# A two-layer encoder trunk on one core: an early gate row, deferred scans, gates split one block ahead, and other buffers for the last adaLN blocks

## The chip, the cores and the metric

The kernel runs on one core of a Trainium2 chip. The metric is the time of one execution in device microseconds (us), the median of several runs. The core has five engines with a queue each: TensorE (PE in the profile; PEld is its weight load), VectorE (DVE), ScalarE (ACT), GpSimd (POOL) and SyncE (SP), which issues most of the loads. An engine takes its queue in order. On-chip memory comes in tiles from pools with a fixed number of buffers. A compile-time scheduler orders the instructions of each engine, by their place in the program and by when it believes that their inputs and buffers are ready. Where the kernel sets an order by hand, the scheduler keeps it.

## The reference

512 tokens of width 1024 go through two layers. Each layer has a token mixer and a SwiGLU FFN of width 2816. Layer 0 mixes by stick-breaking attention with 16 heads, layer 1 by a gMLP with chunked position mixing. Every sub-layer is wrapped in RMSNorms and in adaLN, a shift, scale and gate computed from a condition vector c:

```
m = silu(c) @ w + b;  shift, scale, gate = split(m, 3)
h = rms_norm(x, pre_g) * (1 + scale) + shift
y = mixer(h)            # or swiglu(h)
x = x + gate * rms_norm(y, post_g)
```

In the attention, with z the scores of one head, a weight is beta of its own key times the product of (1 - beta) over the later keys; the kernel gets it as differences of a running product, which one scan along the row gives.

## The kernel before, in words

All matmuls are done in split fp32: an operand x becomes a high part (ACT, "split", L130) and a low part x - high (DVE), and three matmuls replace one (`mm3`, L122). So each weight block of 128x1024 costs one load, one ACT and one DVE instruction of about a microsecond each, and PE has three passes to cover them.

**Weights** come as one stream in the order of use (`stream`, L356 to L391). `wload` (L147) loads the next block into one of two raw buffers, `wemit` (L157) splits it into one of five, later six, buffers, and `wget` (L343) hands a block to the consumer and makes sure that some blocks ahead are emitted ("look", 3 unless told otherwise). The blocks of the FFN that are made of sums (`blocks`, L258) have a second raw block, `rawy`, in a pool of two buffers (tag `raw2`).

**General slots.** The pool `s4` (L45, `slot`, L58) has 28 buffers of 4 KB a partition for everything of middling life: activations, transposed inputs, FFN gates, gate sums, x tiles.

**adaLN in the background.** Three vectors (A scale, B shift, G gate) for each sub-layer are matrix-vector products of c with 1024x1024 blocks. The class `Bg` (L443) does them as a generator, a step at a time between other work: it loads eight blocks (`rawada`), adds each into an accumulator on DVE (`ada_stt`, L436), and at the end, in two halves of 512 columns, splits the accumulator (tiles `acch`, `accl`), sums over the partitions with a matmul against ones, and multiplies with the row of `pre_g` or `post_g` (tile `g`, loaded at that time to all partitions). `bg0` (L708) does G0, `bg` A0 and B0, and `bg2` (L1694) A2 and B2, the last ones. With `slots=0` the blocks go into the two `raw2` buffers, otherwise into general slots.

**Attention.** Heads are done in pairs, i = 0 to 7 (loop L1129 to L1167). In that stage PE and DVE are chained: each engine's instructions keep the program's order (`pe["chain"]`, `dve.chain`). `scores` (L1001) makes scores z, a sigmoid (ACT, tile `ga`) and the scan (DVE, tile `left`) for a group of key blocks: B31 (blocks 3 and 1), B2 and B0. `flip` (L1039) transposes scan blocks on PE (tile `tw`), takes them out on ACT and makes the low part on DVE (tiles `ar`). `values` (L1057) multiplies with the value differences U (tile `av`), `gather` (L1072) adds the two heads' halves (tile `of`), and `part` (L1082) splits the result (tile `o`). Pair i's iteration makes, in between, the scores of pair i+1; the scan of B0 is the last of them, just ahead of the last `values` and `gather`. LATE blocks need the scans of B31 and B2 only; EARLY ones need B0. Between the steps `fill` puts matmuls of the next q and k projections (`pqk`), or for the last pairs of the output projection (`y`). The sigmoid needs another ACT table than the square root of the norms; `sqrt_table` (L703) queues the reload behind `last_act`, the last instruction that needs the old table.

**Output projection and boundary.** `out_proj` (L618) is used after each sub-layer. It runs over the contraction blocks k; after the first FFN (`steps` = 2) the gate product of block k is split first (`act_split`, L1177, tile `as`), background steps are taken after each k, and token tile 0's sum is taken out halfway into `yp` and added at the end. The last four blocks are done token tile by token tile, followed by `boundary` (L539): norm, gate, residual, next norm, transposes on PE (tile `tp`), split (tiles `hTh`, `hTl`). At the end of tiles 2 and 3 the first products of the next sub-layer are put in (`nxt`): after the first FFN these are the v products of the gMLP (`v_first`, L1530), whose weights are `win_v` blocks. Inside tile 3's boundary (`mid`, L681) the flag `edge` orders the splits of `wgu` blocks behind that tile's square (ACT, `feature[1]`) and behind its normed x (DVE, `feature[0]`, tile `t`).

Of the kernel before, what the change touches and what calls it, by code (L numbers as in the profile page):

```python
# [35 lines left out]
def trunk(ctx: ExitStack, tc: tile.TileContext, A: dict, out: bass.AP):  # L36
# [120 lines left out]
    def wemit():  # L157
        n = len(got)
        src, a, b, key = stream[n]
        if len(raws) == n:  # L160
            wload()
        if key[0] == "vblocks":
            got.append(vblocks(raws[n]))
            return
        if src is None:
            if key[1][0] != "u" and (not first_blocks or n > first_blocks[-1] + KF):
                first_blocks.append(n)
            for _ in blocks(*next_raws(n)):
                pass
            return  # L170
        raw = raws[n]
        if key[0] == "wdn" and key[2] in SEVEN[key[1]]:
            got.append(down_blocks(raw))
            return
        h, l = wtile(a, b, SHORT if key[0] in ("wgu", "win_u") else 16)
        if key[0] == "wqk" and key[1]:

            act.activation(h[:], raw[:], AF.Copy)
            nc.vector.tensor_tensor(l[:], raw[:], h[:].bitcast(F32), ALU.subtract)
            if len(raws) == n + 1 and stream[n + 1][3][0] == "wqk":  # L180
                wload()
        else:
            high = act.activation(h[:], raw[:], AF.Copy)
            last_low[0] = nc.vector.tensor_tensor(l[:], raw[:], h[:].bitcast(F32), ALU.subtract)  # L184
# [258 lines left out]
    class Bg:  # L443
# [5 lines left out]
        def __init__(self, *parts, slots=0, lag=None, gap=2, flat=False):  # L449
            self.slots = slots  # L450
# [5 lines left out]
            self.parts = [  # L456
                (n, int(s), int(s) + (n != "G"), {"G": 2, "A": 1, "B": 0}[n]) for n, s in parts
            ]
            self.gen = self.run()

        def run(self):
            groups = [self.parts] if self.flat else [[p] for p in self.parts]
            for group in groups:
                raws = []
                n = KD * len(group)
                for j in range(n + self.lag):
                    if j < n:
# [16 lines left out]
            for name, at, s, part in self.parts:  # L484
                acc = ada[name, at]
                if part:
                    row = A["pre_g"] if part == 1 else A["post_g"]
                    g = slot(F32, "g", 1, D)[:, 0, :]
                    load(g, row[s : s + 1, :].to_broadcast([P, D]))
                for b in range(2):  # L490
                    c = slice(b * 512, (b + 1) * 512)
                    h = adas.tile([P, 512], F32R, tag="acch", name=nm("acch"))
                    l = adas.tile([P, 512], F32R, tag="accl", name=nm("accl"))
                    split(h[:], l[:], acc[:, c])
# [3 lines left out]
                    mm(ps[:], ones_r, h[:], True, False, last_tp[0])  # L498
                    mm(ps[:], ones_r, l[:], False, True)
# [39 lines left out]
    def boundary(s, tt, y, xin, hT, S, tag, mid=None):  # L539
# [4 lines left out]
        for hf, c in enumerate(halves):  # L544
            act.activation(junk[:, c], y[hf][:], AF.Square, accum_out=sq[hf][:])
            if hf == 1:
                sd, r2 = rms(sq[1][:], sq[0][:])
            dve.tensor_tensor(t[:, c], y[hf][:], ada["G", s][:, c], ALU.mult)
# [69 lines left out]
    def out_proj(s, nk, get_act, wkey, J, bg, hT, nxt=(), pre=None, S=None, steps=0, bg2=None):  # L618
# [23 lines left out]
        if pre is not None:  # L642
            npre = len(pre["w"])
            for tt in pre["y"]:
                y[tt] = pre["y"][tt]
        for k in range(nk - J):
            a = get_act(k)
# [14 lines left out]
            (k, get_act(k), wget(wkey(k), J + 1 if k == nk - J else 0))  # L662
# [5 lines left out]
        for tt in range(NT):  # L668
# [11 lines left out]
        for n, tt in enumerate((2, 3)):  # L680
# [5 lines left out]
            if nxt and tt == 2:  # L686
                evacs.append(nxt[0]())
            late.append(
# [19 lines left out]
    bg0, bg = Bg("G0", slots=3, gap=1), Bg("A0", "B0", lag=1, gap=1)  # L708
# [194 lines left out]
    with tc.tile_pool(name="att", bufs=1) as att, tc.tile_pool(name="att2", bufs=2) as att2:  # L903
# [80 lines left out]

        def attend(i):
# [15 lines left out]
            def scores(js):  # L1001
# [24 lines left out]
                if tri is None:  # L1026
                    tri = gaps[B0][0][:, : T - P * js[0]]
                    parts = [slice(o, o + T - P * js[0]) for o in at.values()]
                else:
                    parts = [slice(0, M)]  # L1030
                for c in parts:
                    dve.tensor_tensor_scan(r[:, c], g[:, c], tri, 1.0, ALU.mult, ALU.max)
                for h in range(2):
                    for j in js:
                        weights[h, j] = r, at[h, j]

            turned = {}

            def flip(blocks, h):  # L1039
# [10 lines left out]
                act.activation(ar[:, 0, :n], ps[:, :n], AF.Identity, bias=minus)  # L1050
# [78 lines left out]
        for i in range(NPAIR):  # L1129
# [4 lines left out]
            flip(LATE, 1)  # L1134
            if i:
# [24 lines left out]
            fill(next(F))  # L1160
            if more:
                cur[0](B0)
# [531 lines left out]
    bg2 = Bg("A2", "B2", lag=1, gap=3)  # L1694
# [110 lines left out]
```

## Time and profile before

| | us |
|---|---|
| median of 3 runs | 1102.92 (1102.55 to 1105.05) |
| profiled execution, its own time | 1103.49 |
| its span, first to last instruction | 1101.7 |
| PE busy in the span | 1082.1 |
| DVE busy | 972.8 |
| ACT busy | 610.1 |

The granted TensorE clock was 0.998 on the mean. Timeline rows give start, duration, engine, line, operation, tiles (out<-in), shape and count; in brackets stands the idle time before the row and what ended it. Rows that merge several instructions give the time from the first start to the last end. Since most operations go through helpers, rows are told apart by tiles, not by lines. A row of busy time by stretch gives, after the length, the busy time of PE, PEld, DVE, ACT and POOL with the number of instructions, then the granted clock, the busy share of the DMA engines and the GB/s that they moved. In the list of waits the numbers are the total, how often, and the longest.

### The profile page before, as it was taken

How to read it: one execution, taken by the hardware profiler on the slowest of the kernel's cores; microseconds unless marked ns; L12 is line 12 of the kernel's file. 1: busy time of each engine (PE TensorE's matmuls, PEld its weight loads, DVE VectorE, ACT ScalarE, POOL GpSimd, SP SyncE). 2: the span in 40 equal slices, each digit the busy share in tenths (PEclk: the TensorE clock that was granted, in tenths of full speed). 3: DMA queues.
4: the chain of work that ended last, by engine and by line, in shares of the span. 5: the costliest groups of instructions: out<-in, count | busy, mean ns of one | idle time of the engine just before them, and what ended most of it. 6: DMA issues, size and time to landing. Idle time of an engine off the chain costs nothing.

```text
span 1101.7 us, 18701 instructions
## 1 busy us (share of the span) xinstructions
PE 1082.1 (98%) x7452; PEld 978.7 (89%) x7452; DVE 972.8 (88%) x1293; ACT 610.1 (55%) x1016; POOL 29.5 (3%) x53
## 2 busy tenths in 40 slices
PE   7999999999999999999999999999999999999997
PEld 4787788788999999998888899988999999999996
DVE  4988999866989999989978999868979999899996
ACT  6554665665655555554252767526545555565662
POOL 0020100000000000001000000001000000000000
PEclk9999999999999999999999999999999999999999
DMA  8976434304433434359878324524334342332252
GB/s 317 357 226 218 138 121 131 122 17 153 153 111 124 163 124 153 134 187 347 294 246 322 143 87 137 177 95 163 122 113 153 136 159 100 107 113 96 77 190 78
DMA packets 51355, 176.38 MB, mean 160 GB/s; under 512 B 6074, under 2 KB 9146, under 8 KB 51268
## 3 DMA queue, kind: packets, MB, share of 16 engines
q1 hardware_dynamic: 48708, 166.81, 43.8%
q0 software_dynamic: 2560, 8.39, 2.1%
q8 instruction: 58, 0.95, 0.3%
q14 instruction: 29, 0.24, 0.1%
HBM read 164.69 MB, written 8.39 MB: 157 GB/s over the span
## 4 chain that ended last, share of the span: by engine, by line
PE 85%; DVE 7%; DMA 4%; issue 2%; ACT 2%; SPq 0%; DVEq 0%; ACTq 0%
PE r L111 35%; PE y L111 16%; PE pqk L111 7%; PE X L111 4%; PE gu L111 4%; PE Y L111 3%; PE v L111 3%; PE u L111 2%; PE av L111 2%; PE z L111 2%; PE tw L119 1%; PE Z L111 1%; PE W L111 1%; PE tp L119 1%; DVE wl L184 1%
## 5 line engine op out<-in xcount | busy, mean ns | idle before, releaser
L111 PE MATMUL r<-Sh,wh 128*128 128x256 f32 x640 | 177.3, 277 | 0.6 <-ACT e L89 0.6
L111 PE MATMUL r<-Sl,wh 128*128 128x256 f32 x640 | 177.0, 277 | 0.0
L111 PE MATMUL r<-Sh,wl 128*128 128x256 f32 x640 | 176.9, 277 | 0.0
L89 ACT ACTIVATE wh<-raw 128x1024 fp32r<-128x1024 f32 (+1 forms) x105 | 108.3, 1036 | 101.7 <-DMA raw<-in_wdown 36.1
L111 PE MATMUL y<-wh,as 128*128 128x512 f32 x480 | 150.5, 391 | 0.3 <-DVE svt L73 0.3
L111 PEld LDWEIGHTS r<-Sh,wh 128*128 128x128 f32 x640 | 120.2, 188 | 1.2 <-ACT e L89 1.0
L111 PEld LDWEIGHTS r<-Sl,wh 128*128 128x128 f32 x640 | 120.2, 188 | 0.1
L111 PEld LDWEIGHTS r<-Sh,wl 128*128 128x128 f32 x640 | 120.1, 188 | 0.0
L184 DVE TENSOR_TENSOR wl<-raw,wh 128x1024 fp32r<-128x1024 f32 x79 | 95.9, 1220 | 25.9 <-ACT wh L89 25.7
L73 DVE TENSOR_TENSOR wl<-f,wh 128x1024 fp32r<-128x1024 f32 x95 | 112.9, 1219 | 1.1 <-ACT wh L89 1.1
L89 ACT ACTIVATE wh<-f 128x1024 fp32r<-128x1024 f32 x95 | 100.2, 1055 | 17.3 <-DVE f L73 12.5
L111 PEld LDWEIGHTS y<-wh,as 128*128 128x128 f32 x480 | 90.0, 188 | 19.3 <-issue 0.6
L89 ACT ACTIVATE e<-r 128x256 f32<-128x256 f32 x120 | 45.9, 384 | 102.3 <-PE r L111 100.2
L111 PE MATMUL y<-wl,as 128*128 128x512 f32 x240 | 93.7, 391 | 0.0
L111 PE MATMUL r<-hTh,wh 128*128 128x256 f32 x320 | 88.8, 278 | 0.2 <-DVE gu L73 0.2
L111 PE MATMUL r<-hTh,wl 128*128 128x256 f32 x320 | 88.5, 277 | 0.0
L111 PE MATMUL r<-hTl,wh 128*128 128x256 f32 x320 | 88.5, 277 | 0.0
L111 PEld LDWEIGHTS r<-hTh,wh 128*128 128x128 f32 x320 | 60.1, 188 | 1.1 <-DVE gu L73 0.9
L111 PE MATMUL r<-hTh,b 128*128 128x256 f32 x320 | 60.9, 277 | 0.0
L111 PEld LDWEIGHTS r<-hTl,wh 128*128 128x128 f32 x320 | 60.1, 188 | 0.0
L111 PEld LDWEIGHTS r<-hTh,wl 128*128 128x128 f32 x320 | 60.1, 188 | 0.0
L89 ACT ACTIVATE wh<-rawx 128x1024 fp32r<-128x1024 f32 x40 | 42.5, 1062 | 29.7 <-PE r L111 28.9
(288 smaller groups left out, 2924.3 us busy)
## 6 DMA issues: line engine op xcount, KB each, us to landing
rawada<-in_ada SPq DMA_DIRECT2D x80, 512.0 KB, 6.3
rawy<-in_wy SPq DMA_DIRECT2D x38, 512.0 KB, 4.2
rawx<-in_wx SPq DMA_DIRECT2D x38, 512.0 KB, 3.4
raw<-in_wdown SPq DMA_DIRECT2D x22, 512.0 KB, 5.3
raw<-in_wdn SPq DMA_DIRECT2D x22, 512.0 KB, 3.4
raw<-in_wqk SPq DMA_DIRECT2D x16, 512.0 KB, 4.0
ada<-in_ada0p SPq DMA_DIRECT2D x12, 512.0 KB, 7.6
raw<-in_wgu SPq DMA_DIRECT2D x12, 512.0 KB, 3.5
```

The lines of the kernel that those rows point to most:

```text
L73: b = getattr(nc.vector, op)(*args, **kw)
L89: b = nc.scalar.activation(*args, **kw)
L111: b = nc.tensor.matmul(o, l, r, start=start, stop=stop, skip_group_check=True)
L119: last_tp[0] = nc.tensor.transpose(o, i, ident)
L184: last_low[0] = nc.vector.tensor_tensor(l[:], raw[:], h[:].bitcast(F32), ALU.subtract)
```

## The change

Six things are changed.

- **G0's row and halves** (`soon=True` for `bg0`). The row g is loaded right behind the eighth block instead of at the end. The two halves of the accumulator are split at once, the second into a general slot of its own.
- **Scans deferred.** For pairs 6 and 7 (made in iterations 5 and 6) the scan of B0 is left out of `scores` and done in the next iteration, behind both LATE flips and ahead of `last_part`.
- **Table reload later.** In the last iteration `last_act` is set to the last `ar` of the LATE flips, so the square-root table is loaded behind it.
- **Gates one block ahead.** In `out_proj` with `steps`, the gates of block k+1 are split before the weights of block k are asked for.
- **Last adaLN blocks in general slots.** `bg2` (`own=0`) takes general slots for its blocks.
- **Edges after the first FFN.** The two halves of `yp` are added inside the boundary as they are asked for, each with an order: the first behind the last weight's low part, the second behind DVE's instruction before it. `win_v` splits are ordered behind the boundary's square and normed x as `wgu` ones are, and the flag is also set for the products put in at tile 2.

```diff
-            if edge[0] and key[0] == "wgu":
+            if edge[0] and key[0] in ("wgu", "win_v"):
...
+        def row(self, name, s, part):
+
+            if part and name not in self.rows:
+                g = slot(F32, "g", 1, D)[:, 0, :]
+                row = A["pre_g"] if part == 1 else A["post_g"]
+                load(g, row[s : s + 1, :].to_broadcast([P, D]))
+                self.rows[name] = g
+            return self.rows.get(name)
...
-                        if self.slots:
+                        if self.slots or len(self.raws) >= self.own:
                             raw = slot(F32, "rawada", 1, D)[:, 0, :]
...
+                        self.raws.append(raw)
+                        if self.soon and j % KD == KD - 1:
+                            self.row(name, s, part)
...
+                g = self.row(name, s, part)
+                halves = []
                 for b in range(2):
                     c = slice(b * 512, (b + 1) * 512)
...
+                    if not (self.soon and b):
+                        h = adas.tile([P, 512], F32R, tag="acch", name=nm("acch"))[:]
+                        l = adas.tile([P, 512], F32R, tag="accl", name=nm("accl"))[:]
+                        split(h, l, acc[:, c])
+                        halves.append((h, l))
+                    if self.soon and not b:
+                        s = slot(F32R, "acc")
+                        split(s[:, 0, :], s[:, 1, :], acc[:, 512:])
+                        halves.append((s[:, 0, :], s[:, 1, :]))
+                    h, l = halves[b]
...
         for k in range(nk - J):
-            a = get_act(k)
+            a = act_at(k)
+            if steps:
+                act_at(k + 1)
             w = pre["w"][k] if k < npre else wget(wkey(k))
...
-                for hf in range(2):
-                    dve.tensor_tensor(yp[:, hf, :], y[tt][hf][:], yp[:, hf, :], ALU.add)
-                y[tt] = [yp[:, hf, :] for hf in range(2)]
+                ends = y[tt]
+
+                def added(hf):
+                    before = dve.prev if hf else last_low[0]
+                    b = dve.tensor_tensor(yp[:, hf, :], ends[hf][:], yp[:, hf, :], ALU.add)
+                    order(b, before)
+                    return yp[:, hf, :]
+
+                y[tt] = added
...
             if nxt and tt == 2:
+                edge[0] = steps > 0
                 evacs.append(nxt[0]())
+                edge[0] = False
...
-    bg0, bg = Bg("G0", slots=3, gap=1), Bg("A0", "B0", lag=1, gap=1)
+    bg0, bg = Bg("G0", slots=3, gap=1, soon=True), Bg("A0", "B0", lag=1, gap=1)
...
-            def scores(js):
+            def scores(js, later=False):
...
+                if not later:
+                    scan()
+                return scan
...
             flip(LATE, 0)
             flip(LATE, 1)
+            if scan is not None:
+                scan()
+            if not more:
+                last_act[0] = last_ar[0]
             if i:
                 last_part()
...
+            scan = None
             if more:
-                cur[0](B0)
+                scan = cur[0](B0, i > 4)
+                if i < 5:
+                    scan = None
...
-    bg2 = Bg("A2", "B2", lag=1, gap=3)
+    bg2 = Bg("A2", "B2", lag=1, gap=3, own=0)
```

`act_at(k)` is `get_act(k)` kept in a table, so that each block is split once; `scan()` holds the scan instructions that stood in `scores`.

More of the change, by code (lines that the diff above doesn't have):

```diff
@@ L983, in trunk @@
                 False: [att.tile([P, 544], F32, name=nm("left"))]}
+        last_ar, scan = [None], None
         def attend(i):
@@ L1035, in scores, with scan @@
                         weights[h, j] = r, at[h, j]
+                def scan():
+                    if tri is None:
+                        ones = gaps[B0][0][:, : T - P * js[0]]
+                        parts = [slice(o, o + T - P * js[0]) for o in at.values()]
+                    else:
+                        ones, parts = tri, [slice(0, M)]
+                    for c in parts:
+                        dve.tensor_tensor_scan(r[:, c], g[:, c], ones, 1.0, ALU.mult, ALU.max)
+                if not later:
+                    scan()
+                return scan
             turned = {}
```

37 lines of the change are left out of this document (15 added, 22 removed).

## The prediction

> **What bounds the kernel now.** I read the page's busy times, then busy time by stretch, then the list of what TensorE (PE) waited for, then the timelines around those waits.
>
> ```profile
> PE 1082.1 (98%) x7452; PEld 978.7 (89%) x7452; DVE 972.8 (88%) x1293; ACT 610.1 (55%) x1016; POOL 29.5 (3%) x53
> ```
> ```profile
> 0.00:25.00 25.00, 16.95 (x77) 9.59 (x77) 10.03 (x27) 16.39 (x32) 1.19 (x6) 1.00 0.82 318
> ...
> 1075.00:1100.00 25.00, 19.63 (x101) 16.48 (x99) 18.08 (x32) 5.61 (x16) 0.00 (x0) 0.93 0.24 81
> ```
> PE is idle for 1101.7 - 1082.1 = 19.6 us. The first 25 us hold 25 - 16.95 = 8.05 of it, the last stretch 5.37, the 1.7 us behind it all of theirs. Only 4.5 us of idle lie in the 1050 us between. No edit touches the two ends, so whatever the change gives comes out of these 4.5 us.
>
> ```profile
> PE av L111 <- DVE accl L73: 1.1, 1, 1.1
> PE av L111 <- DVE ar L73: 0.8, 1, 0.8
> PE r L111 <- ACT e L89: 0.6, 1, 0.6
> PE av L111 <- ACT ar L89: 0.4, 1, 0.4
> ...
> PE tp L119 <- DVE t L73: 0.3, 1, 0.3
> PE y L111 <- DVE svt L73: 0.3, 1, 0.3
> ```
> The list of waits names them (total, times, longest). Four lie where the diff works: accl (the background sum of gate G0), both ar waits (the last pairs of heads) and t (the boundary after the first FFN): 1.1 + 0.8 + 0.4 + 0.3 = 2.6 us. Idle time understates a stall, because a matmul's modelled end overlaps the next start; distances between starts show it whole:
>
> ```profile
> 93.59 0.40 PE L111 MATMUL pqk<-hTh,wl 128*128 128x512 f32 x1
> 93.82 0.39 PE L111 MATMUL av<-acch,ones 128*128 128x512 f32 x1
> 95.31 0.50 PE L111 MATMUL av<-accl,ones 128*128 128x512 f32 x1 [1.10 <-DVE accl L73]
> ```
> Neighbours start 0.23 apart, these two 1.49: the stall is 1.26 us, not 1.10.
>
> **The change, part by part.**
>
> *G0's row and halves.* On DVE:
>
> ```profile
> 87.78 0.69 DVE L73 TENSOR_TENSOR accl<-G,acch 128x512 fp32r<-128x512 f32 x1
> ...
> 93.97 0.69 DVE L73 TENSOR_TENSOR G<-av,g 128x512 f32<-128x512 f32 x1 [0.82 <-DMA g<-in_post_g]
> 94.58 0.68 DVE L73 TENSOR_TENSOR accl<-G,acch 128x512 fp32r<-128x512 f32 x1
> ```
> The second half's accl stands behind the product with g in DVE's written order, and that product waits for g's load. After, both halves are split together: the second accl comes 0.7 us behind the first, near 88.5, five us before PE asks. The 1.26 us go, even if g should come late. No instruction is added; the second pair of halves takes one general slot.
>
> The load of g (512 KB) moves up SP's queue, from 85.93 to behind the eighth block of G0:
>
> ```profile
> 42.88 4.25 SPq L128 DMA_DIRECT2D rawada<-in_ada  x5
> 55.62 2.70 SPq L128 DMA_DIRECT2D ones<-in_consts  x6
> ```
> ```profile
> 45.00:50.00 5.00, 4.77 (x21) 3.62 (x20) 4.86 (x9) 1.68 (x3) 0.00 (x0) 1.00 1.03 416
> ...
> 55.00:60.00 5.00, 5.00 (x23) 4.13 (x22) 4.96 (x5) 1.98 (x4) 3.05 (x8) 1.00 0.39 98
> ```
> SP issues nothing from 47.1 to 55.6, so no queue slot is taken from anyone. The DMA engines are full (share 1.03) until 50; at 416 GB/s the row takes 0.524 MB / 416 = 1.26 us. I cost it at nothing: the blocks ahead of it are only for G0's sum, which is done long before its accl at 87.78, and from 55 the share is 0.39. Without that cover it would be 1.26 us, once. [...] From 47 on g holds a general slot that A's blocks or the q and k tiles may want; PE waits for none of these before 93.
>
> Does PE's lead of 1.26 us survive? DVE is its partner through the eight pairs of heads, and it is nearly full. The tightest place, and the next one at which DVE waits:
>
> ```profile
> 125.13 1.02 DVE L73 SCALAR_TENSOR_TENSOR ar<-tw,ar 128x384 fp32r<-128x384 f32 x2
> ...
> 145.38 2.30 DVE L73 TENSOR_TENSOR_SCAN left<-ga,ones 128x1027 f32<-128x1027 f32 x1 [1.07 <-ACT ga L89]
> ```
> ```profile
> 126.99 1.08 PE L111 MATMUL av<-ar,U 128*128 128x128 f32 x8
> ```
> DVE's first ar ends near 125.65 and PE reads it at 127.1; the second ends at 126.15 and is read near 127.6. Slack 1.4 against 1.26: it holds, by a little. At 145 DVE waits 1.07 us for ACT's sigmoid of PE's scores, which would come earlier; DVE follows PE again from there. I carry the lead at its full 1.26.
>
> *Scan of pair 6 deferred.* Before:
>
> ```profile
> 216.39 2.28 DVE L73 TENSOR_TENSOR_SCAN left<-ga,ones 128x1025 f32<-128x1025 f32 x1
> ...
> 220.00 1.02 DVE L73 SCALAR_TENSOR_TENSOR ar<-tw,ar 128x384 fp32r<-128x384 f32 x2
> ...
> 224.56 1.02 DVE L73 SCALAR_TENSOR_TENSOR ar<-tw,ar 128x384 fp32r<-128x384 f32 x2
> ```
> ```profile
> 217.34 1.05 ACT L89 ACTIVATE ar<-tw,oneb 128x384 fp32r<-128x384 f32 x2
> ```
> ```profile
> 219.61 0.22 PE L111 MATMUL av<-ar,U 128*128 128x128 f32 x1
> 220.62 1.08 PE L111 MATMUL av<-ar,U 128*128 128x128 f32 x7 [0.79 <-DVE ar L73]
> ...
> 225.97 1.08 PE L111 MATMUL av<-ar,U 128*128 128x128 f32 x8
> ```
> The eight av matmuls start 0.11 apart; the second comes 1.01 late to the first: a stall of 0.90. With the 2.28 us scan behind it, DVE's ar follows ACT's at 218.4 and is done by 219.4, before PE's 219.7: the 0.90 go. But the scan is not gone. The timeline shows no pause of DVE between this scan and the next ar's end at 225.58, and the new order adds one, from the old start of the scan until ACT has delivered. PE, now 0.90 earlier, asks for that next ar near 225.1 instead of 225.97. So part is given back there: between nothing and all 0.90. I take the middle, a net 0.45.
>
> *Scan of pair 7 deferred, square-root table later.*
>
> ```profile
> 230.66 1.28 ACT L705 ACT_TABLE_LOAD   x1
> ...
> 233.19 1.05 ACT L89 ACTIVATE ar<-tw,oneb 128x384 fp32r<-128x384 f32 x2
> ```
> ```profile
> 233.00 0.40 PE L111 MATMUL y<-wh,o 128*128 128x512 f32 x1
> 233.83 0.33 PE L111 MATMUL av<-ar,U 128*128 128x128 f32 x1 [0.42 <-ACT ar L89]
> ```
> The table load sits ahead of the ar for which PE waits; the stall is 0.83 - 0.23 = 0.60. After, the load follows that ar, which comes 1.28 us sooner, and DVE's half no longer stands behind a scan. All 0.60 go. Next on ACT is the split of o, now 1.28 us behind the load; the output projection wants it only after the remaining fills. No further pair follows, so DVE owes nothing here.
>
> *Boundary after the first FFN.*
>
> ```profile
> 598.11 1.28 DVE L73 SCALAR_TENSOR_TENSOR B<-rawada,sc,B 128x1024 f32<-128x1024 f32 x1 [1.95 <-DMA rawada<-in_ada]
> ```
> ```profile
> 605.32 0.64 ACT L89 ACTIVATE b<-rawy 128x512 fp32r<-128x512 f32 x1 [1.45 <-DMA rawy<-in_wuy]
> ```
> The last blocks of A2 and B2 go through two buffers that the rawy loads share; DVE waits for them up to the edge, and a late rawy puts ACT's b in front of the square of x on which tile 0 hangs. In general slots both come sooner, and PE's wait for t goes: 0.26 (0.3 in the list). Adding the two halves of yp in turn keeps the order that DVE had anyway. Splitting the gates one block ahead: PE has no wait on them in this stage, nothing to win; two halves each on ACT and DVE (0.69 on DVE for this shape, as accl's row) move up one block, and one slot more is held. PE's block of 24 x 0.23 = 5.5 us hides them; without it, 1.4 us would show once, at the stage's start.
>
> *win_v's weights behind the boundary.* The block that tile 2's edge orders is no later than before. The last one is ordered by tile 3's:
>
> ```profile
> 625.17 1.21 DVE L184 TENSOR_TENSOR wl<-raw,wh 128x1024 fp32r<-128x1024 f32 x1
> ...
> 631.34 1.28 DVE L73 SCALAR_TENSOR_TENSOR t<-t,r,B 128x1024 f32<-128x1024 f32 x1
> ```
> ```profile
> 629.88 0.39 PE L111 MATMUL v<-wl,hTh 128*128 128x512 f32 x1
> ```
> PE reads this wl at 629.88. Behind t it ends at 632.62 + 1.21 = 633.83 if nothing else moves: 3.95 late. With the wl away, t itself comes about 1.2 sooner, so 2.75. Against that, this stretch of PE is not ordered by hand: v of token tile 2 (24 matmuls, 5.4 us) and u are ready work. Bounds 0 and 3.95; I take 0, the value of the nearest row: this read had no wait. Queued behind the waiting split are, on ACT, win_u's split and, on DVE, the sums of tiles 2 and 3; the raw buffer comes free later by as much, so SP's load of wvs behind it starts later too. PE needs none of these before it has used the last win_v block. The rest of the bound is a rival.
>
> **Sum.** 1.26 + 0.45 + 0.60 + 0.26 = 2.57 us. Against the profiled execution's own time, 1103.49 (its span of 1101.7 and 1.79 around it), that is 1100.9. That execution lies 0.57 above the median of the runs, 1102.92; from the median, 1100.4. With the give-back at its ends, 1099.9 to 1100.8; with some scatter of the schedule 1099.8 to 1101.2.
>
> **Rivals.** About 0.2% (2.2 us, a time under 1100.7) can be told from no change.
> 1. *win_v stalls PE.* For: the rows above. Against: ready work. If half covered, 1 to 2 us: 1101.4 to 1102.4. If PE's order was fixed without that cover, 4 to 5 us with the transposes of tile 3, which are ordered behind these matmuls: 1104.4 to 1105.4, slower than before. It decides above 2.6 us of stall.
> 2. *DVE eats the lead.* For: its slack is 1.4 us against 1.26, and it is full from 214. Then pair 6's 0.45 and pair 7's 0.60 are left of the first three terms, with the boundary 1.31: 1101.6.
> 3. *General slots run out.* SP stands in order behind a load without a buffer:
>
> ```profile
> 536.72 10.17 SPq L128 DMA_DIRECT2D rawada<-in_ada  x4
> ```
> ```profile
> raw<-in_wdown SPq DMA_DIRECT2D x22, 512.0 KB, 5.3
> ```
> SP stood 10.17 us over four such loads. A wdown load lands 5.3 us after its issue, and its two splits take about 1.2 each (wl above). Weights run three blocks ahead, 3 x 24 matmuls x 0.23 = 16.5 us, so 8.8 are spare. A slot of the gates comes free every two blocks, 11 us: a PE stall of about 2.2 us a time. Three of them take 6.6, and 1100.4 becomes 1107; it decides at two. Against: blocks of FFN gates come free all the while. [...]
> 4. *Neighbouring waits go too*, r's 0.6 and y's 0.3, as work shifts: 1099.5.
>
> **How the numbers follow.** Forecast 0.54 (two thirds of it below 1100.7); rival 1 covered by half 0.14, in full 0.06; rival 2 0.09; rival 3 0.06; rival 4 0.11. Faster: 0.37 + 0.11 = 0.48. Slower: half of the full rival 1, and rival 3: 0.09. Same: 0.43. The range runs from rival 4 with no give-back, 1099.0, to the upper half-covered rival 1 with the scatter of the runs, 1103.0.
>
> **What would show it.** Right: no PE wait on accl near 94; g issued near 47; the av wait of pair 6 gone and a small one near 225; the table load behind ar; tile 0's transposes without a wait. Wrong: a PE gap at v before 633, SP standing over 9 us in front of a wdown load, new ar waits between 100 and 215.

## The result, and the profile after

The kernel after takes 1110.36 us, the median of 6 executions (1108.83 to 1110.89), against 1103.91 (1102.15 to 1105.11) for the kernel before beside it: 1.0057 times as long, interval 1.0044 to 1.0070. The forecast was 1100.4, and a range of 1099.0 to 1103.0. The profiled execution took 1108.83, its span 1107.1.

The page's first line, then the list of what PE waited for (total, times, longest):

```profile
PE 1083.8 (98%) x7452; PEld 979.1 (88%) x7452; DVE 972.4 (88%) x1293; ACT 610.7 (55%) x1016; POOL 29.5 (3%) x53
```
```profile
PE v L111 <- ACT wh L89: 3.3, 1, 3.3
PE z L111 <- ACT ga L89: 1.5, 1, 1.5
PE tp L119 <- DVE t L73: 0.5, 1, 0.5
...
PE av L111 <- DVE ar L73: 0.2, 1, 0.2
```

PE's idle time is 1107.1 - 1083.8 = 23.3 us, 3.7 more than before. Of the four waits that were to go, accl's and ACT's ar are gone, DVE's ar is down to 0.2, t has grown. The two new ones together, 4.8, are larger than all that went, 2.1. Where the time went shows best when the same matmul is looked up in both traces (starts in us):

| matmul | before | after | difference |
|---|---|---|---|
| first score, z | 72.56 | 73.09 | +0.53 |
| 31st q and k fill | 95.65 | 94.82 | -0.82 |
| first transpose of pair 0's scans, tw | 102.45 | 101.66 | -0.79 |
| first av of the LATE blocks of pair 6 | 219.61 | 218.82 | -0.79 |
| first FFN product, gu | 277.47 | 277.50 | +0.02 |
| first y of the FFN | 493.85 | 492.70 | -1.15 |
| first v of the gMLP | 620.59 | 619.84 | -0.76 |
| last v | 646.88 | 652.59 | +5.71 |
| last of all | 1094.24 | 1099.57 | +5.34 |

The second last step holds the result: 6.47 us between the first and the last v. The timeline there (PE, ACT, DVE):

```profile
628.76 0.40 PE L111 MATMUL v<-wh,hTl 128*128 128x512 f32 x1
...
630.35 1.06 ACT L89 ACTIVATE junk<-x 128x1024 bf16<-128x1024 f32 x1 [1.95 <-DVE x L73]
...
631.40 1.04 ACT L89 ACTIVATE wh<-raw 128x1024 fp32r<-128x1024 f32 x1
...
632.50 1.22 PE L111 MATMUL v<-wh,hTh 128*128 128x512 f32 x2 [3.34 <-ACT wh L89]
```

PE has no v without win_v's last block; the high part, wh, stands behind the square of tile 3's x (junk), as the change orders it. Starts that would be 0.23 apart are 3.74 apart: 3.51 us. Busy time by stretch shows what follows; the number behind the five engines is the granted clock:

```profile
628.00:630.00 2.00, 1.16 (x5) 0.58 (x4) 2.00 (x4) 0.40 (x1) 0.00 (x0) 1.00 0.00 0
630.00:632.00 2.00, 0.00 (x0) 0.00 (x0) 2.00 (x4) 1.65 (x3) 0.53 (x1) 0.87 0.11 43
632.00:634.00 2.00, 1.50 (x3) 0.87 (x4) 1.95 (x4) 1.98 (x4) 0.00 (x0) 0.50 0.53 219
...
636.00:638.00 2.00, 2.00 (x6) 1.58 (x5) 0.42 (x1) 0.00 (x0) 0.00 (x0) 0.50 0.78 244
638.00:640.00 2.00, 2.00 (x9) 1.57 (x8) 0.00 (x0) 0.48 (x1) 0.00 (x0) 0.93 0.82 264
```

After the idle stretch the clock is 0.50 until 638, and v matmuls start 0.43 apart in place of 0.23: the starts between 632.50 and 638.4 hold 2.96 us more than at full clock. 3.51 + 2.96 = 6.47.

The other new wait is at the deferred scan of pair 6:

```profile
218.32 2.28 DVE L73 TENSOR_TENSOR_SCAN left<-ga,ones 128x1025 f32<-128x1025 f32 x1
...
220.72 1.21 ACT L89 ACTIVATE ga<-z 128x128 f32<-128x128 f32 x4 [2.60 <-DVE left L73]
...
221.43 0.50 PE L111 MATMUL z<-acch,ones 128*128 128x512 f32 x1 [1.54 <-ACT ga L89]
```

ACT's next sigmoids write `ga`, which the late scan has yet to read; they are what frees the bank of z, and PE's background sum needs that bank. By distances between starts it is 1.70, in the place of 0.90.

At G0 the step worked, at a price. The row was issued where predicted, the two halves follow each other and PE does not wait for them; but a weight's low part comes 0.76 later than before (66.38 against 65.62), since ACT takes the q and k tiles 3 us later:

```profile
47.29 0.33 SPq L128 DMA_DIRECT2D g<-in_post_g  x1
...
67.66 0.50 PE L111 MATMUL v<-wl,hTh 128*128 128x512 f32 x1 [0.40 <-DVE wl L184]
...
88.22 0.68 DVE L73 TENSOR_TENSOR accl<-G,acch 128x512 fp32r<-128x512 f32 x1
...
94.36 0.63 PE L111 MATMUL av<-acc,ones 128*128 128x512 f32 x2
```

### The profile page after: what moved, and what is told of

Read it like the earlier page. It is cut to its first block, busy times and chain, and to the rows that moved or that the text cites. A ratio compares the mean times of both kernels' runs of the same rounds, so it can differ in the third digit from the quotient of the medians.

```text
span 1107.1 us, 18698 instructions
## 1 busy us (share of the span) xinstructions
PE 1083.8 (98%) x7452; PEld 979.1 (88%) x7452; DVE 972.4 (88%) x1293; ACT 610.7 (55%) x1016; POOL 29.5 (3%) x53
## 5 line engine op out<-in xcount | busy, mean ns | idle before, releaser
L184 DVE TENSOR_TENSOR wl<-raw,wh 128x1024 fp32r<-128x1024 f32 x79 | 95.8, 1219 | 23.9 <-ACT wh L89 23.3
```

## The experiments

Each kernel was timed beside the kernel before, and ratios are to that. Traces of one and the same code differ by over a microsecond in places: up to the first score the kernels without G0's edit lie between 1.5 us ahead of before's and 1.1 behind, those with it between 0.3 ahead and 2.4 behind. accl's stall at 94, 1.26 in before, is 0.6 to 1.9 in the kernels that leave it alone, and PE's wait for t at tile 0 of the boundary, 0.42 in before by starts, is 0.73 to 2.75 in the seven that change nothing there. Four of the traces below (fifteen matmuls in the gap, the order at tile 2's edge only, after without the gates ahead, after without win_v's order and without those blocks) also have a slow clock near 222 that after's does not have; it is worth 1.6 us and is taken up in the last section. So a place is judged by the distance from one matmul to a later one, and by starts that lie further apart than their neighbours'.

**Theory A:** win_v's order makes PE stand 3.5 us, and the idle stretch halves its clock. **Rivals:** the adaLN blocks in general slots make the weights late (B), the deferred scans (C), another part of the change (D).

### The gap at v

**After without win_v's order**

```diff
-            if edge[0] and key[0] in ("wgu", "win_v"):
+            if edge[0] and key[0] == "wgu":
```

> The kernel after, with only the loads of the FFN gates, and not win_v's, ordered behind the boundary's sums (as before). Theory (win_v's order costs what was lost): in the trace of after PE's matmuls of v stop at 628.76 and resume at 632.50, and run at a granted clock of 0.50 until 638; from the first gmlp v to the last PE falls back by 0.76 + 5.71 = 6.5 us against before. Without it the time is 6 to 6.5 us below after, 1103.9 to 1104.4, or 0.4 us below before (what is left of the other edits' gain at the end of attention and FFN, 0.76 us, minus small losses). Rival (last blocks of bg2 in general slots push the FFN's weight loads 5 us later, and PE waits for those): no more than 1 us below after; the gap before 633 stays. Rival (the deferred scans): the loss would show before 240 us; nothing changes here, 1110.

Measured: 1.0024 (1.0014 to 1.0034). From the first v to the last PE loses 0.31 against before in place of 6.47: the gap is gone. Yet only 0.33%, 3.6 us, came back. The trace loses 3 us at a place where after lost none:

```profile
710.25 1.06 ACT L89 ACTIVATE wh<-raw 128x1024 fp32r<-128x1024 f32 x1 [1.52 <-DMA raw<-in_wout]
...
715.32 0.39 PE L111 MATMUL sv<-ws,vnh 128*128 128x256 f32 x1 [1.24 <-ACT u L89]
...
716.63 0.61 PE L111 MATMUL y<-wh,as 128*128 128x512 f32 x1 [0.64 <-DVE svt L73]
```
```profile
718.00:720.00 2.00, 2.00 (x6) 1.59 (x6) 2.00 (x6) 0.63 (x1) 0.00 (x0) 0.50 0.99 383
```

A late load of the out projection's weights holds ACT's split; DVE's half of it starts at 711.34, and DVE's product u, the splits of that product and of the next weight, and ACT's u queue up behind, until 715.27. PE waits 1.35 and 0.75 by its starts, and the clock halves again. A is right on the gap; the sum has a second term.

**The order at tile 2's edge only**

```diff
-            if edge[0] and key[0] in ("wgu", "win_v"):
+            if edge[0] and key[0] == "wgu" or edge[0] == 2 and key[0] == "win_v":
...
-                edge[0] = steps > 0
+                edge[0] = 2 if steps > 0 else False
```

> The kernel after, with win_v's block ordered behind the boundary at tile 2's edge only; the one at tile 3's edge is free again. Theory (the last block, at tile 3's edge, is what PE stands for): as the run without win_v's order, 1.001 to 1.0025 of before, no gap at v before 633. Rival (tile 2's block pushes everything behind it): the gap stays, 1.005.

Measured: 1.0033 (1.0021 to 1.0044); no gap at v, and the second loss is there as in the kernel without the order at either edge. The block at tile 3's edge is the one, as the prediction had it.

**Fifteen matmuls in the gap**

```diff
+                if j == 3:
+                    pe["chain"] = True
+                    idle = bank("idle")
+                    for _ in range(15):
+                        mm(idle[:], ones_r, v0["w"][0][0][:, 0, :], True, True)
...
+            pe["chain"] = False
```

The result of these matmuls is not used; the chain keeps PE's instructions in the order written there.

> The kernel after with 15 matmuls more (a row of ones by a block of win_v, 128x512, 3.4 us at 0.227 each, result unused), ordered between the third and the fourth block of v of tiles 2 and 3, so that PE is busy where it waited 3.3 us in after. Theory (half of the loss is the clock, which the idle stretch halves): the wait for the weights stays, but the matmuls behind it start 0.227 apart from the first on: 2.5 to 3.2 us below after, some 1107.5, clock 0.95 or more from 630 to 640. Rival (the clock falls for another reason, say because the load on PE changes there, or the slow matmuls wait for data): no change against after, or slower by up to 3.4 us.

Measured: 1.0041 (1.0027 to 1.0054), some 1.7 us below after's 1.0057, with intervals that overlap. The trace is plainer: a wait is left behind the added work, but no slow clock.

```profile
631.10 3.66 PE L111 MATMUL idle<-wh,ones 128*128 128x512 f32 x15
634.63 0.49 PE L111 MATMUL v<-wh,hTh 128*128 128x512 f32 x1
...
635.75 0.39 PE L111 MATMUL u<-hTh,wh 128*128 128x256 f32 x1 [0.63 <-ACT wh L89]
```
```profile
636.00:638.00 2.00, 2.00 (x11) 1.67 (x11) 2.00 (x3) 1.00 (x1) 0.00 (x0) 1.00 0.00 0
```

First to last v costs 4.46 in place of 6.47. So the slow clock in after comes from the idleness (from 636 to 638 it is 1.00 with the work put in, 0.50 without), and holds nearly half of the loss, 2.96 of 6.47 by the starts in after.

**win_v's order alone**

```diff
-            if edge[0] and key[0] == "wgu":
+            if edge[0] and key[0] in ("wgu", "win_v"):
```

> The kernel before, with win_v's split ordered behind the boundary's sums at the edge, and nothing else of the change. Theory: slower by 5 to 6.5 us, 1109 to 1110.5, with PE's gap of 3 us or more at v and a clock of 0.5 behind it. Rival (bg2's shift of the loads makes the gap, the order alone finds its weights in time): within 1 us of before. Between the two: a gap shorter than in after, with no fall of the clock, would be 2 to 3.5 us slower.

Measured: 1.0017 (1.0006 to 1.0027), between the theories' figures. Its trace, of the slowest of its executions (1109.31), is no help: PE comes to v 4.15 late, after waiting for t at tile 0, and then finds its weights almost in time.

**win_v's order and the last blocks in general slots**

```diff
-            if edge[0] and key[0] == "wgu":
+            if edge[0] and key[0] in ("wgu", "win_v"):
...
-    bg2 = Bg("A2", "B2", lag=1, gap=3)
+    bg2 = Bg("A2", "B2", lag=1, gap=3, own=0)
```

> The kernel before with win_v's order and with the last raw blocks in general slots, nothing else. Theory (the order costs 3.3 us of wait and some 2 to 3 us of slow clock when PE comes to v on time, and less when a wait at tile 0 has made PE late; with the blocks in general slots tile 0's wait is small): gap at v of 3 us or more, clock 0.5 behind it, 1.004 to 1.006 of before. Rival (the order alone is worth 1.9 us, the rest of after's loss is of other parts): 1.002 or less.

Measured: 0.9996 (0.9986 to 1.0006). First to last v costs 0.00 against before. A falls as it was put: the order alone doesn't make the gap.

```profile
625.25 1.28 DVE L73 SCALAR_TENSOR_TENSOR x<-t,r,x 128x1024 f32<-128x1024 f32 x1
...
628.77 2.00 ACT L89 ACTIVATE wh<-raw 128x1024 fp32r<-128x1024 f32 x2
```

Tile 3's x starts 3.84 behind the first v (621.41); in before 5.70 (626.29 - 620.59), in after 9.20 (629.04 - 619.84):

```profile
626.29 1.28 DVE L73 SCALAR_TENSOR_TENSOR x<-t,r,x 128x1024 f32<-128x1024 f32 x1
```
```profile
629.04 1.27 DVE L73 SCALAR_TENSOR_TENSOR x<-t,r,x 128x1024 f32<-128x1024 f32 x1
```

In after the sums of the tiles run late against PE, and win_v stands behind the last of them. They are late from tile 0 on:

```profile
597.07 6.98 SPq L128 DMA_DIRECT2D raw<-in_win_v  x3
...
601.38 1.06 ACT L89 ACTIVATE wh<-raw 128x1024 fp32r<-128x1024 f32 x1 [3.18 <-DMA raw<-in_win_v]
602.47 1.23 DVE L184 TENSOR_TENSOR wl<-raw,wh 128x1024 fp32r<-128x1024 f32 x1 [3.02 <-ACT wh L89]
603.62 0.68 DVE L73 TENSOR_TENSOR yp<-y,yp 128x512 f32<-128x512 f32 x1
```

That is the timeline of after: the first half of yp is written behind the low part of win_v's second block, DVE stands 3.02 us for that, and its load was issued at 597.07 (591.61 in before). Two parts of the change meet there, so each was taken out.

**After without the order of yp**

```diff
-            yh = y(hf) if callable(y) else y[hf][:]
+            yh = y[hf][:]
...
-                ends = y[tt]
-
-                def added(hf):
-                    before = dve.prev if hf else last_low[0]
-                    b = dve.tensor_tensor(yp[:, hf, :], ends[hf][:], yp[:, hf, :], ALU.add)
-                    order(b, before)
-                    return yp[:, hf, :]
-
-                y[tt] = added
+                for hf in range(2):
+                    dve.tensor_tensor(yp[:, hf, :], y[tt][hf][:], yp[:, hf, :], ALU.add)
+                y[tt] = [yp[:, hf, :] for hf in range(2)]
```

> The kernel after with the two halves of yp added as in before, without a written order; win_v's order and all else stay. Theory (yp behind the split of a block whose load is late makes all four tiles late, and win_v's last block stands behind the fourth): tile 0's sum starts 2 to 3 us sooner, tile 3's x comes 4 to 6 us behind PE's first v in place of 9.2, PE's gap at v is gone or under 1 us, no slow clock: 1.000 to 1.002 of before, 4 to 6 us below after. Rival (the gates ahead do it): the gap stays, 1.005.

Measured: 1.0001 (0.9991 to 1.0010), 6 us below after. yp's first half is added ahead of the split of win_v's second block, which is as late as in after:

```profile
600.12 0.69 DVE L73 TENSOR_TENSOR yp<-y,yp 128x512 f32<-128x512 f32 x1 [0.74 <-PE y L111]
...
604.42 1.22 DVE L184 TENSOR_TENSOR wl<-raw,wh 128x1024 fp32r<-128x1024 f32 x1 [0.16 <-ACT wh L89]
...
625.76 1.28 DVE L73 SCALAR_TENSOR_TENSOR x<-t,r,x 128x1024 f32<-128x1024 f32 x1
```

Tile 3's x is 4.4 behind the first v (621.38), and of the gap 0.38 us is left. Nor does the second loss near 714 come.

**After without the gates ahead**

```diff
             a = act_at(k)
-            if steps:
-                act_at(k + 1)
```

> The kernel after with the FFN's gates split in their own block, as in before; win_v's and yp's orders and all else stay. Theory (the order of yp is the cause, the gates are not): the gap at v stays at 2 us or more, 1.004 or more of before. Rival (the gates ahead change the order of PE and DVE at the boundary, alone they cost 1.0010): the gap is gone, 1.002 or less.

Measured: 1.0016 (1.0007 to 1.0025); the rival is right as well. The gap shrinks to two waits of 0.34 and 0.38:

```profile
594.33 6.67 SPq L128 DMA_DIRECT2D raw<-in_win_v  x3
...
599.43 1.23 DVE L184 TENSOR_TENSOR wl<-raw,wh 128x1024 fp32r<-128x1024 f32 x1 [1.25 <-ACT wh L89]
600.57 0.68 DVE L73 TENSOR_TENSOR yp<-y,yp 128x512 f32<-128x512 f32 x1
```

yp is still behind that split, but the load is issued 2.74 earlier, so yp starts 3.05 earlier. **The gap takes three parts at once:** gates ahead (a late load, and that only with the blocks in general slots, as shown below), yp's order (the tiles behind that load), win_v's order (PE's weights behind the tiles). Without any one of them the waits at v are under 0.8 us. A kernel with these three and without the blocks in general slots was not run.

**Gates ahead alone**

```diff
+            if steps:
+                act_at(k + 1)
```

> The kernel before with the FFN's gates split one block ahead, nothing else. Prediction's step: no difference, since PE waits for none of these splits. Rival (one slot more held brings SP and the weights later, or the other order of DVE costs at the boundary): 1 us or more above before.

Measured: 1.0010 (1.0000 to 1.0019), at the edge of what can be told.

**The last blocks in general slots alone**

```diff
-    bg2 = Bg("A2", "B2", lag=1, gap=3)
+    bg2 = Bg("A2", "B2", lag=1, gap=3, own=0)
```

> The kernel before with the last raw blocks of A2 and B2 in general slots, nothing else. In after their loads moved up to 531 to 543, and the weight loads of the boundary came about 5 us later than before, so that tile 0's sums were later, not sooner. Theory (this edit costs at the boundary): PE's wait for t at tile 0 stays or grows by 0.2 to 2 us; time from 0.2 below to 2 us above before. Prediction's step: rawy and the blocks come sooner, the wait of 0.26 goes, 0.3 below before. Rival for the whole result (this edit, not the order of win_v, makes PE stand at v before 633): 4 us or more above before, with that gap.

Measured: 0.9994 (0.9985 to 1.0004), no difference; rival B falls as the sole cause. win_v's first load is issued 4 us later (592.85 against 588.81), and PE's stalls for t are 0.23 and 0.30 in place of before's 0.42.

**After without win_v's order and without those blocks**

```diff
-            if edge[0] and key[0] in ("wgu", "win_v"):
+            if edge[0] and key[0] == "wgu":
...
-    bg2 = Bg("A2", "B2", lag=1, gap=3, own=0)
+    bg2 = Bg("A2", "B2", lag=1, gap=3)
```

> The kernel after without win_v's order and with the last raw blocks of A2 and B2 in their own two buffers as before. Theory (those blocks in general slots bring win_u's last load and the loads of wout 5 us later once PE is on time, and PE then waits for sv): the wait of 1.4 to 1.5 us near 711 to 714 and the slow clock behind it are gone, 2 to 3 us below the run without win_v's order alone, 1.000 of before. Rival (another part makes that second loss): unchanged, 1.002.

Measured: 1.0004 (0.9996 to 1.0012). The waits near 714 are gone: with win_v free the blocks in general slots were worth the other 2 us. Why they bring the out projection's weights later was not taken apart.

On win_v's late load the traces of all these kernels, put side by side, say more. Counted from the first v, the second block's load is issued 29.0 us ahead in before. With the gates ahead and the blocks in their old buffers (the gates alone, and the kernel just shown) it is 29.7 to 30.0. With the blocks in general slots and no gates ahead it is 25.4 to 26.0, and with both, in after and five others, 22.4 to 23.2. So the gates delay this load only together with those blocks. The delay begins at a load of wdown. In after SP stands 18.1 us in front of it, until DVE's split of an earlier block has freed the raw buffer; with the blocks in general slots alone of the two it stands 13.3 to 14.5 there, and before's longest stand in that stage is 7.9:

```profile
550.37 0.34 SPq L128 DMA_DIRECT2D rawada<-in_ada  x1
568.80 0.33 SPq L128 DMA_DIRECT2D raw<-in_wdown  x1
```

PE shows no stall in that stage. Why the split itself comes so late was not taken apart.

### Attention

**G0's row and halves alone** (`row` and `halves` as in the change)

```diff
-    bg0, bg = Bg("G0", slots=3, gap=1), Bg("A0", "B0", lag=1, gap=1)
+    bg0, bg = Bg("G0", slots=3, gap=1, soon=True), Bg("A0", "B0", lag=1, gap=1)
```

> The kernel before with the row g of G0 loaded early and both halves split at once; nothing else. In the trace of after PE was 1.35 us ahead behind the old stall at 94, but had lost 0.56 on the way there (0.53 behind before at the first q and k fill), and was 0.8 ahead through attention. Theory: 0.5 to 0.9 us below before. Prediction's step: 1.26 below before. Rival (the lead is lost to DVE in the pairs of heads or later): no difference.

Measured: 0.9992 (0.9979 to 1.0005), which holds the theory's 0.5 to 0.9 us, the prediction's 1.26 and nothing at all. In the trace 1.36 us are won by the 31st fill and the new 0.59 at 67 is there.

**The deferred scans alone**

```diff
+            if scan is not None:
+                scan()
...
-                cur[0](B0)
+                scan = cur[0](B0, i > 4)
```

> The kernel before with the scans of pairs 6 and 7 deferred, nothing else. Theory (the one buffer of the sigmoids): the 0.9 us stall of av near 220 goes, but ACT's next sigmoid waits for the deferred scan to have read ga, PE's background fill waits for ACT, and 1.5 to 1.7 us appear near 221; pair 7's 0.6 go only in part. From the first av of pair 6 to the last av of the stage PE is 0.1 to 0.3 us faster or slower than before: no difference in time. Prediction's step: 0.45 below before (0.90 less half). Rival (the deferral itself is free, the loss came from elsewhere in after): 0.9 to 1.5 below before.

Measured: 1.0012 (1.0003 to 1.0020): it costs. From the first av of pair 6 to the last av PE loses 0.96, and the wait is after's:

```profile
219.12 2.28 DVE L73 TENSOR_TENSOR_SCAN left<-ga,ones 128x1025 f32<-128x1025 f32 x1
...
221.51 1.21 ACT L89 ACTIVATE ga<-z 128x128 f32<-128x128 f32 x4 [2.60 <-DVE left L73]
...
222.23 0.50 PE L111 MATMUL z<-acch,ones 128*128 128x512 f32 x1 [1.53 <-ACT ga L89]
```

**The deferred scans with a buffer of their own**

```diff
                 tri, at, M = gaps[js]
+                gs, ga = (slot(F32, "gb", 1, D)[:, 0, :], {(h, 0): h * T for h in range(2)}) if later else (g, at)
...
-                            o, n = at[h, j], T - P * j
+                            o, n = ga[h, j], T - P * j
...
-                                g[:, o : o + n], zb[h][:, offs[j] : offs[j] + n], AF.Sigmoid, scale=-1.0
+                                gs[:, o : o + n], zb[h][:, offs[j] : offs[j] + n], AF.Sigmoid, scale=-1.0
```

and the scan reads `gs` in two pieces.

> As the run with the deferred scans alone, but the sigmoids whose scan is deferred write a general slot of their own in place of ga, and the scan reads that in two pieces of 512 in place of one of 1025. Theory (one buffer of the sigmoids is what takes the gain back): no wait of z on ga near 221, av without a wait near 220: PE 0.9 to 1.5 us sooner at the last av than in the run with the deferred scans alone, and 0.9 to 1.5 below before in time. Rival (DVE's order, not the buffer, gives it back): the wait moves to the next ar, near 225, and nothing is gained against that run.

Measured: 0.9982 (0.9974 to 0.9990), 3.3 us below the one without the buffer. ACT no longer waits for the scan:

```profile
217.26 1.22 ACT L89 ACTIVATE ga<-z 128x128 f32<-128x128 f32 x4
217.45 2.33 DVE L73 TENSOR_TENSOR_SCAN left<-gb,ones 128x512 f32<-128x512 f32 x2
...
218.87 0.39 PE L111 MATMUL z<-acch,ones 128*128 128x512 f32 x1
```

PE wins 0.65 over this stretch: the 0.90 less a stall of 0.26 at z near 223. The buffer is the cause of the wait. The traces put 1.6 of the 3.3 us in this stretch (0.96 lost, 0.65 won); the rest is open, since the wait for t at tile 0, which neither edit touches, also differs by 1.9 us between the two.

**The table's move alone**

```diff
+            if not more:
+                last_act[0] = last_ar[0]
```

> The kernel before with the square-root table loaded behind the last ar of ACT, nothing else. In before PE stands 0.6 us at 233.8 behind that ar; in after 0.27 and 0.36 are left there, on DVE's ar and left. Theory: 0 to 0.6 below before, that is too little to tell from none in time, and the anchors show it: last av 0.2 to 0.6 sooner.

Measured: 0.9993 (0.9983 to 1.0003), no difference. ACT's ar is early now, but DVE's half stands behind the scan; PE's stall grew from 0.60 to 1.32 (0.46 and 0.86):

```profile
229.76 2.29 DVE L73 TENSOR_TENSOR_SCAN left<-ga,ones 128x1025 f32<-128x1025 f32 x1 [1.15 <-ACT ga L89]
231.97 1.38 DVE L73 TENSOR_TENSOR of<-av,of 64x512 f32<-64x512 f32 x2
...
234.00 1.07 PE L111 MATMUL av<-ar,U 128*128 128x128 f32 x7 [0.65 <-DVE ar L73]
```

**G0 and the buffered scans; the same with the table; and that with the row at its old place.** The edits shown above together; the third leaves out

```diff
-                        if self.soon and j % KD == KD - 1:
-                            self.row(name, s, part)
```

> The kernel before with G0's row early and both halves at once, and with the deferred scans reading a slot of their own; no other part of the change. Theory (the two gains are at different places and each carries to the end): 0.9992 x 0.9982 of before, 0.9974, some 2.8 us less. Rival (DVE, nearly full through attention, eats the lead of the first before the second): 0.9982, no more than the second alone.

> As the run before it in this lot, with the square-root table loaded behind ACT's last ar as well. In the run with the table alone the wait of av near 232 grew from 0.60 to 1.32 us, because DVE's half of ar came behind its scan; with that scan deferred 0.63 was left in after, on DVE's ar and left. Theory: within 0.5 us of the run without the table's move, 0.997 of before. Prediction's step (all 0.6 go): 0.6 us below it.

> As the run with G0, the own slot for the deferred sigmoids and the table's move, but G0's row g is loaded at its old place; its halves are still split at once. Theory (the early row's slot makes the q and k tiles, and by them the split of a weight, late): the 0.57 us that every run with the early row shows at 67 are gone, and the stall at 94 stays gone, so 0.5 us less than that run, 0.9971 of before. Rival (the halves' own slot does it, or the row is then late): 0.57 stays, or accl's wait comes back, up to 1.3 us above that run.

Measured: 1.0001 (0.9990 to 1.0013), 0.9976 (0.9965 to 0.9986) and 0.9981 (0.9972 to 0.9990). The first misses both of its figures and stays open. The table's move is worth 0.33 in the traces (pair 7's stall 0.59, then 0.27); the rest of the 2.8 us between these two is not explained by it. With the row at its old place the 0.57 at 67 goes and 0.68 at 98 comes, where a fill waits for DVE's q: no gain, so the early row costs nothing on balance. The second is the best kernel found, 0.24% below before.

**After, mended in two places**

```diff
-            if edge[0] and key[0] in ("wgu", "win_v"):
+            if edge[0] and key[0] == "wgu":
...
+                gs, ga = (slot(F32, "gb", 1, D)[:, 0, :], {(h, 0): h * T for h in range(2)}) if later else (g, at)
```

> The kernel after, mended in its two places: win_v's split not ordered behind the boundary, and the sigmoids whose scan is deferred in a slot of their own. Theory (these two make up the loss): against the run without win_v's order (1.0024 of before) the 1.7 us of z at 221 go, so 1.0 to 1.7 us less: 1.0010 to 1.0015 of before, or below 1 if the 3 us that that run's trace lost near 714 (a wait of sv for ACT, then a slower clock) do not come again. Rival (the last raw blocks in general slots or the gates ahead cost as well): stays at 1.002 or above.

Measured: 0.9993 (0.9983 to 1.0003), below what the theory gave, though its trace still loses some 3 us from 711 on, to the same two waits and the slow clock behind them.

## Why the prediction was wrong

- **G0.** Right where it looked: the 1.26 went (1.35 in the trace), g was issued at 47, and nothing is seen waiting for g. The slot that g holds was named and put aside because "PE waits for none of these before 93"; by way of the q and k tiles and a weight's split PE did wait, at 67, 0.56 us; with the row at its old place that wait is gone. That it is the slot, and not the load, which does this was not tried apart. Net 0.8.
- **The lead** survived attention: -0.82 at the 31st fill, -0.79 at pair 6. Rival 2 did not happen.
- **Pair 6**, net 0.45 to be won: 0.80 lost. The step gave back time only through DVE's order, and bounded that by the 0.90 won. It followed the deferred scan to what comes after it on DVE, not to the buffer that it still had to read and to the writer that waits for this buffer.
- **Pair 7**, 0.60: after has 0.27 and 0.36 left, at DVE's ar and at left. Next in line was DVE. With the own buffer the stall is 0.27, so 0.33 is what this step is worth.
- **Boundary**, 0.26 by idle time, 0.42 by starts: t's stall was 0.64 in after, which its scatter from trace to trace (0.42 to 2.75) doesn't tell from no change. The blocks did come sooner; that the weights' loads come later with them was not followed.
- **win_v, gates and yp**, each taken at 0: together 6.5 us. This is the step that failed. It took the lower end, because ready work of tile 2 would cover a late block. None did: PE ran nothing from 628.76 to 632.50, and the first u came at 633.63, behind the v that were waited for. The prediction named this case (rival 1, 1104.4 to 1105.4) and gave it 0.06. Its price was short too: the 3.95 was reckoned from before's timeline, where the tiles are 3.5 us earlier against PE, and the clock was left out. Tried alone, the gates measured 1.0010 and win_v's order 1.0017 (0.9996 with the blocks in general slots), near the 0 that they were given; the order of yp was not tried alone. They were costed one by one, on a trace in which the other two had not happened.
- **Rival 3's sign**, SP standing over 9 us in front of a wdown load, came (18.1 us), but SP waited for DVE's split of a weight, not for a general slot, and PE did not wait there. What came of it was win_v's late load.
- **Rival 4** came true in part: r's wait at 317 is gone in after, which with smaller things is worth 1.2 us from the first gu to the first y of the FFN.

By the anchors of the first table: +0.53 (up to the first score) - 1.35 (G0) + 0.03 (up to pair 6) + 0.81 (pairs 6 and 7, up to the first gu) - 1.17 + 0.39 (up to v) + 6.47 - 0.37 = 5.34, which is the difference of the two profiled executions, 1108.83 - 1103.49.

## What to carry to other kernels

When an instruction is deferred, follow not only its own engine but every buffer that it still reads: the next writer waits, and so does whoever waits for that writer (behind pair 6's scan ACT stood 2.60 us, PE 1.54, or 1.70 by its starts). Orders written by hand multiply: one that waits for a load, one behind which a chain stands, and one that puts weights behind that chain cost 2 us or less where they were tried singly and 6.5 us together, so cost them on the timeline that the other edits leave. Where a wait could leave PE idle for as long as the stands here, 1.70 to 3.51 us, put the slow clock behind it into the price, at least as a rival: 1.70 us was followed by a clock of 0.50 in four traces of eight.

## What the hardware showed that was not expected

In after the slow clock cost nearly as much as the wait, 2.96 us beside 3.51, and shorter stands were followed by it too: one of 2.87 us with win_v's order alone, and 1.35 and 0.75 us with 0.45 of work between in after without win_v's order; but in the kernel with the deferred scans alone a stand of 2.75 was not. Busy time by stretch, first of the kernel with win_v's order alone, behind its wait at 608 to 611, then of the one with the deferred scans alone, behind its wait at 609 to 612:

```profile
614.00:616.00 2.00, 2.00 (x6) 1.54 (x5) 2.00 (x3) 1.69 (x4) 0.53 (x1) 0.50 0.00 0
```
```profile
614.00:616.00 2.00, 2.00 (x10) 1.66 (x9) 1.97 (x4) 1.50 (x3) 0.00 (x1) 1.00 0.00 0
```

The wait of 1.70 us behind pair 6's deferred scan stands in eight traces. In four of them the clock was then half, y matmuls started 0.43 apart in place of 0.23, and PE lost 1.6 us more (the four named under The experiments); in the other four it stayed full (after, after without win_v's order, after without the order of yp, the deferred scans alone). First after, then after without the gates ahead:

```profile
222.00:224.00 2.00, 2.00 (x13) 1.55 (x11) 2.00 (x1) 1.79 (x4) 0.00 (x0) 1.00 0.00 0
```
```profile
222.00:224.00 2.00, 2.00 (x9) 1.75 (x8) 2.00 (x3) 0.93 (x3) 0.00 (x0) 0.50 0.00 0
```

What decides whether and when the clock falls was not shown: the same 1.70 us went with a fall in four traces and without one in four. Of the moments this much is measured: in after's trace the clock was half for 6.827 us, and in the clock records of before and after each change lies a whole number of times half of that, 3.4133 us, behind the first record: in after at 617.81 us (181 times), 624.64 (183) and 1088.85 (319), in before at 1082.03 (317).
